# Two orders of small work in a mixture-of-experts stage, and the place of one constant's load

## The chip, the cores and the metric

The kernel runs on one core of a Trainium2 chip. The metric is device time in microseconds (us) of one execution. TensorE (PE) multiplies matrices, VectorE (DVE) and ScalarE (ACT) work element by element, GpSimd (POOL) does a few small steps, and SyncE (SP) issues nearly all DMA transfers; POOL issues some.

## The reference, cut to what matters

A decoder trunk of two layers on 256 tokens of width 1024, in float32. Each layer is a mixer (`w_in`, three head groups, `w_out`) and a feed-forward part: dense in layer 0, eight experts in layer 1, of which each token uses two.

```python
def _swiglu(t, w_g, w_u, w_d):
    return (jax.nn.silu(t @ w_g) * (t @ w_u)) @ w_d

def _moe(h, w_router, w_g, w_u, w_d):
    ...
    logits = (t @ w_router).astype(jnp.float32)
    top_v, top_i = lax.top_k(logits, TOP_K)
    top_w = jax.nn.softmax(top_v, axis=-1)
    gates = jnp.sum(jax.nn.one_hot(top_i, N_EXPERTS, dtype=jnp.float32) * top_w[..., None], axis=1)
    out = jnp.zeros(t.shape, jnp.float32)
    for e in range(N_EXPERTS):
        out = out + gates[:, e:e + 1] * _swiglu(t, w_g[e], w_u[e], w_d[e]).astype(jnp.float32)
    return out.astype(h.dtype).reshape(B, S, D)
```

Ahead of the router stands an RMS norm with weights of its own (1024 numbers), and a final norm follows the last layer.

## The kernel before

**Weights.** The experts' weights come as 264 chunks of 1 MB, 33 for each expert (11 of gate, 11 of up, 11 of down). Each chunk goes through four steps: a DMA from SP's queue into `w`, `wx` or a borrowed area (line 148), a rounded copy `wr` by ScalarE and the rest `wl = w - wr` by VectorE (`split`, lines 125 and 127), and matmuls with both halves. Float32 precision comes from three products for an even expert (lines 184 to 186, 12 matmuls a chunk) and from two for an odd one, whose tokens' two halves lie side by side (lines 887, 888, 956, 957; 8 matmuls a chunk). Every fourth chunk uses `wrx` and `wlx`, the others share a ring of three. So a chunk's split can start when TensorE is done with the chunk four before. A chunk's split is written in the program three chunks ahead of its matmuls (`AHEAD = 3`).

**Pairs.** The experts are ranked by their number of tokens and handled in pairs: expert 2p with 128 rows, 2p + 1 with 64 rows (`FEW`); what doesn't fit is left to a loop at the end (`rest`). The chunks of the odd expert run `LAG = 2` steps behind those of the even one, and the two are interleaved, gate, up and down, in the loop over `j`.

**Small tasks.** Between chunks run small tasks, the `jobs`:
- for pair 0 `count`, `order`, `assign` (which sets the ids from which SP addresses the later experts' weights), `where`, `shares` and `limits`, all short steps on VectorE;
- `marks`, one-hot matrices of a pair's tokens (VectorE, line 807, tile `xg`);
- `factors`, the tokens' shares (4 matmuls into `rgb`, line 841, then VectorE); `back`, transposed marks (TensorE into `ptb`, ScalarE out of it);
- `pick`, four a pair: gathers two of the eight slices of the tokens (8 matmuls into `gb`, line 821), and splits them into `xg`. For pairs 1 to 3 that is ScalarE, VectorE, ScalarE, VectorE; for pair 0 only the odd expert's columns are left to do, by one step on each;
- `scale` (two an expert), the expert's result times its shares into `yg`, and `finish` (four an expert), which scatters it (`cb`) and adds it to `h` (VectorE, line 977);
- `space` only takes memory.

`chunk()` appends a chunk to the list `prog` and then takes one job from the front of `jobs`. New jobs are put at the end when an expert's last down chunk is listed (`lower`), and when the memory of a pair is free (`collect`). Ahead of an even expert's first chunk all `pick` jobs still in the list, and what stands ahead of them, are listed at once. What is left at the end of the loop follows the last chunk. `in_order()` then fixes the order of the instructions of TensorE, VectorE and ScalarE as they were written. So the order of jobs is the order in which the engines meet them, and an engine that waits for one holds all behind it.

Before the change, the chunk numbers behind which the jobs stand are: pair 0, chunks 0 to 12; pair 1, chunks 30 to 39 (`space`, two `marks`, two `factors`, `back`, four `pick`); pair 2, 94 to 103; pair 3, 160 to 169; `scale` and `finish` of expert 6, 255 to 260. Expert 2's first chunk is 52, expert 4's 118, expert 6's 184, and the last chunk is 263.

**Constants.** `late_consts()` is called in layer 0's mixer; it starts the loads of `wa2` and `stg` from POOL's queue. `moe()` opens with the tile `gains`, the norm's weights repeated on all 128 partitions (512 KB), and its load from POOL's queue; POOL multiplies by it in front of the router.

Of the kernel before, what the change touches and what calls it, by code (L numbers as in the profile page):

```python
# [8 lines left out]
F32 = mybir.dt.float32  # L9
# [8 lines left out]
P = 128  # L18
T = 256
TT = 2  # L20
D = 1024
# [24 lines left out]
K_GAIN = K_TRI + 128  # L46
# [66 lines left out]
def trunk_kernel(ctx: ExitStack, tc: tile.TileContext, x, w_in, w_out, dense_w_gate, dense_w_up, dense_w_down,  # L113
                 moe_w_gate, moe_w_up, moe_w_down, final_norm_g, consts, decay_w, out):
    nc = tc.nc
# [4 lines left out]
    mix = early.enter_context(tc.tile_pool(name="mix", bufs=1))  # L120
# [72 lines left out]
    def tmp(shape, name, tag="tmp", bufs=5, dt=F32):  # L193
        pool = area["scratch"] if tag in ("tmp", "u", "cf_acc", "S", "r", "v", "gy", "qk", "sx", "kept", "fold", "rt_f") else sb
        return pool.tile(shape, dt, name=name, tag=tag, bufs=2 if tag == "tmp" and area["spare"] else bufs)

    def bank(shape, name):
        return ps.tile(shape, F32, name=name, tag="ps")
# [22 lines left out]
    mk = mix.tile([P, NL, P], U8, name="mk")  # L221
    mst = mix.tile([P, 9, P], F32R, name="mst")
    wa2 = mix.tile([17, 2, 256], F32, name="wa2")

    cr = cp.tile([P, 2, P], F32R, name="cr")
    oner, trir = cr[:, 0], cr[:, 1]
# [2 lines left out]
    def late_consts():  # L229
        nc.gpsimd.dma_start(wa2, decay_w)  # L230
        stg = tmp([P, 11 + NL, P], "stg", tag="E", bufs=1)
        nc.gpsimd.dma_start(stg, consts[:, K_M:K_GAIN].rearrange("p (l q) -> p l q", q=P))
        return stg

    def cast_consts(stg):
# [94 lines left out]
    def mixer(l, accs):  # L330
# [26 lines left out]
        if l == 0:  # L357
            stg = late_consts()
# [285 lines left out]
        return accs  # L644

    def moe(l, j, accs):
        gains = mix.tile([P, D], F32, name="gains")
        nc.gpsimd.dma_start(gains, bass.AP(tensor=consts.tensor, offset=consts.offset + K_GAIN, ap=[[0, P], [1, D]]))
        fh = tmp([P, 2, KT * T], "fh", tag="A", bufs=1)
        ft = fh[:, 0].rearrange("p (k t) -> p k t", k=KT)  # L650
        hg = fh[:, 1].rearrange("p (t d) -> p t d", t=TT)
# [80 lines left out]
        def places():  # L732
            cnt, rank, idf, few, room = (tmp([P, NE], n, tag="rt_" + n, bufs=1)
                                         for n in ("cnt", "rank", "idf", "few", "room"))
            w0 = cmp[:, 0, 0:NE]
            w1 = cmp[:, 1, 0:NE]
            to = cmp[:, 0, NE:2 * NE]
            V = nc.vector

            def count():  # L740
                nb = bank([P, NE], "nb")
                for tt in range(TT):
                    nc.tensor.matmul(nb, oner, msk[:, tt], start=(tt == 0), stop=(tt == 1))
                V.tensor_copy(cnt, nb)

            def order():
                lte = lt.rearrange("p (a b) -> p a b", b=NE)
                mine = cnt[:, :, None].broadcast_to([P, NE, NE])
                V.tensor_tensor(w0, cnt[:, None, :].broadcast_to([P, NE, NE]), mine, op=ALU.subtract)
                V.scalar_tensor_tensor(w1, w0, 0.0, lte, op0=ALU.is_equal, op1=ALU.mult)  # L750
                V.scalar_tensor_tensor(w0, w0, 0.0, w1, op0=ALU.is_lt, op1=ALU.add)
                V.tensor_reduce(rank, w0[:, :, 1:NE], axis=AX.X, op=ALU.add)
                V.memset(rank[:, 0:1], -1.0)

            def assign():
                V.tensor_tensor(to, target[:, :, None].broadcast_to([P, NE, NE]),
                                rank[:, None, :].broadcast_to([P, NE, NE]), op=ALU.is_equal)
                V.tensor_tensor(w0, to, iota[:, None, 0:NE].broadcast_to([P, NE, NE]), op=ALU.mult)
                V.tensor_reduce(idf, w0, axis=AX.X, op=ALU.add)
                V.tensor_scalar(ids, idf, -1.0, None, op0=ALU.add)  # L760

            def move(tt, src, dst):
                V.tensor_tensor(w0, to, src[:, None, :].broadcast_to([P, NE, NE]), op=ALU.mult)
                V.tensor_reduce(dst, w0, axis=AX.X, op=ALU.add)

            def where():
                for tt in range(TT):
                    move(tt, pos[:, tt], placed[:, tt])

            def shares():  # L770
                for tt in range(TT):
                    move(tt, gr[:, tt, :, 0], gp[:, tt, :, 0])
                V.tensor_copy(gp[:, :, :, 1], rs[:, :, None].broadcast_to([P, TT, NE]))
                V.tensor_tensor(folded, ident[:, 0:FEW], ident[:, FEW:P], op=ALU.add)

            def limits():
                V.tensor_scalar(few, rank, -0.5, None, op0=ALU.is_gt)
                V.scalar_tensor_tensor(few, rank, 3.5, few, op0=ALU.is_lt, op1=ALU.mult)
                V.tensor_scalar(room, few, float(FEW - P), float(P), op0=ALU.mult, op1=ALU.add)
                V.tensor_tensor(over, pos, room[:, None, :].broadcast_to([P, TT, NE]), op=ALU.subtract)  # L780
                V.tensor_tensor(few, cnt, room, op=ALU.subtract)
                V.tensor_scalar(few, few, 0.0, None, op0=ALU.max)
                V.tensor_reduce(nmax, few, axis=AX.X, op=ALU.max)

            return count, order, assign, where, shares, limits
# [73 lines left out]
        def width(c):  # L859
            return 512 if c < 5 else 256  # L860

        jobs = []

        def chunk(e, src, n, a, b, fn):
            prog.append(((e, src, n, a, b), fn))
            if jobs:
                step(*jobs.pop(0))

        def step(fn, *args):
            prog.append((None, partial(fn, *args)))  # L870

        def proj(which_src, e, c):
# [18 lines left out]
            for k0 in range(0, KT, kn):  # L891
                chunk(e, src, 2 * c + k0 // kn, kn, n, partial(run, k0))
# [89 lines left out]
        def item(kind, k):  # L982
            return items[kind][k] if 0 <= k < len(items[kind]) else None

        def lower(it):
            if it is None:
                return
            e, c = it
            for k2 in range(width(c) // 256):
                down(e, c, k2)  # L990
            if c == 5 and e < NE - 1:
                jobs.extend([(scale, e, (0,)), (scale, e, (1,))])
                jobs.extend((finish, e, (tt,), (nh,)) for nh in range(2) for tt in range(TT))
                if e % 2 == 1 and e < NE - 3:
                    collect(e // 2 + 2)

        def collect(p):
            jobs.extend([(space, p), (marks, p, 0), (marks, p, 1)])
            jobs.extend([(factors, p, 0), (factors, p, 1), (back, p)])
            jobs.extend((pick, p, 0, P + FEW, (k2,)) for k2 in range(KT // 2))  # L1000

        jobs.extend((fn,) for fn in places())
        jobs.extend([(marks, 0, 1), (factors, 0, 1), (back, 0)])
        jobs.extend((pick, 0, P, P + FEW, (k2,)) for k2 in range(KT // 2))
        n_pairs = len(items[0]) + LAG
        for j in range(n_pairs + 2):
            hv, hv1 = item(0, j), item(0, j - 1)
            lt_, lt1, lt2 = (item(1, j - LAG - d) for d in range(3))
            closing = j == n_pairs - 1
            if j == 4:  # L1010
                collect(1)
            if hv and hv[1] == 0 and j:
                while any(job[0] is pick for job in jobs):
                    step(*jobs.pop(0))
            if hv:
                drain = proj(0, *hv)
                if j == 0:
                    step(factors, 0, 0)
                step(drain)
            if lt1:  # L1020
                step(fold, *lt1)
            if j == 1:
                step(turn, *hv1)
            if not closing:
                lower(lt2)
            if lt1:
                step(unfold, *lt1)
            if hv:
                step(proj(1, *hv))
            if lt_:  # L1030
                step(proj(0, *lt_))
            lower(hv1)
            if hv and j:
                step(turn, *hv)
            if lt_:
                step(proj(1, *lt_))
            if closing:
                lower(lt2)
# [115 lines left out]
    accs = dense_ffn(0, 0, accs)  # L1154
    accs = mixer(1, accs)
    nmax, rest, close = moe(1, 0, accs)

    def final(close=None):
# [52 lines left out]
```

## Time and profile before

| | |
|---|---|
| time, median of 3 runs | 1185.08 us (1184.42 to 1187.38) |
| profiled execution | 1185.49 us, span of its trace 1183.5 us |
| mean granted TensorE clock | 0.985 |
| TensorE busy | 1138.0 us (96%) |
| VectorE, ScalarE busy | 990.5, 789.5 us |
| experts' first chunk starts | 450.26 us |
| first matmul of the last chunk | 1168.39 us |

The rows below are of the profiled execution. `start us` counts from the start of the span. A releaser in brackets is what ended the idle time in front of an instruction, and a clock of 1.00 is the full one. Neighbouring instructions of one kind are merged in a timeline's row (`x4`); then the time is that of all of them.

### The profile page before, as it was taken

The page shows a single profiled execution, that of the slowest core. Times are in us where ns is not written, and L with a number is a line of the kernel's source. Part 1 is how long each engine was busy: PE and PEld are TensorE (multiplying, and loading weights), DVE is VectorE, ACT ScalarE, POOL GpSimd, SP SyncE. Part 2 cuts the span into 40 slices and gives each one's busy share as a digit, 9 for nine tenths or more (in the row PEclk, how much of TensorE's full clock was granted, in tenths as well). Part 3 has the DMA queues.
Part 4 walks back from the last instruction along what each step waited for, and adds up shares of the span by engine and source line. Part 5 has one row for each costly group of instructions (what it writes and reads, how often), then busy time and mean ns, then how long its engine had stood idle before and what let it go on. Part 6 is the DMA issues. An engine that isn't in the chain of part 4 may idle for free.

```text
span 1183.5 us, 17163 instructions
## 1 busy us (share of the span) xinstructions
PE 1138.0 (96%) x6633; PEld 992.4 (84%) x6633; DVE 990.5 (84%) x1065; ACT 789.5 (67%) x801; POOL 28.0 (2%) x36
## 2 busy tenths in 40 slices
PE   6999999999899999899999999899999899999995
PEld 6998999999899978788888888788888788888883
DVE  4998655555679876799799999799999799999996
ACT  4754544334455466587688887688887788887874
POOL 2001000000000120000000000000000000000000
PEclk9999999999999998999999999999999999999999
DMA  9333555455433455898799999799999799999991
GB/s 374 128 138 146 191 189 191 179 183 180 155 129 140 179 218 210 321 373 314 265 416 423 408 424 385 284 400 424 402 424 382 293 411 423 401 424 401 425 403 38
DMA packets 48934, 348.97 MB, mean 295 GB/s; under 512 B 5447, under 2 KB 5447, under 8 KB 7120
## 3 DMA queue, kind: packets, MB, share of 16 engines
q1 hardware_dynamic: 48384, 345.50, 74.2%
q0 software_dynamic: 464, 2.33, 0.5%
q8 instruction: 54, 0.88, 0.3%
q14 instruction: 32, 0.26, 0.1%
HBM read 346.76 MB, written 1.05 MB: 294 GB/s over the span
## 4 chain that ended last, share of the span: by engine, by line
PE 80%; DVE 10%; issue 4%; ACT 4%; DMA 1%; POOL 0%; SPq 0%; POOLq 0%; DVEq 0%; ACTq 0%
PE gu L184 9%; PE gu L185 9%; PE gu L186 9%; PE acc_y L184 6%; PE acc_y L185 6%; PE acc_y L186 6%; DVE wl L127 5%; PE gu L888 5%; PE gu L887 5%; PE fb L929 3%; PE acc_y L956 3%; PE acc_y L957 2%; ACT wr L125 2%; DVE wlx L127 2%; PE sbk L443 1%
## 5 line engine op out<-in xcount | busy, mean ns | idle before, releaser
L127 DVE TENSOR_TENSOR wl<-w,wr 128x2048 fp32r<-128x2048 f32 (+2 forms) x267 | 464.1, 1759 | 76.9 <-ACT wr L125 76.5
L125 ACT ACTIVATE wr<-w 128x2048 fp32r<-128x2048 f32 (+2 forms) x267 | 391.9, 1491 | 187.5 <-issue 112.1
L127 DVE TENSOR_TENSOR wl<-wx,wr 128x2048 fp32r<-128x2048 f32 x54 | 122.9, 2284 | 13.4 <-ACT wr L125 13.3
L185 PE MATMUL gu<-wl,xg 128*128 128x512 f32 (+1 forms) x296 | 111.8, 378 | 2.1 <-DVE wl L127 2.1
L184 PE MATMUL gu<-wr,xg 128*128 128x512 f32 (+1 forms) x296 | 113.3, 383 | 0.4 <-ACT wr L125 0.4
L186 PE MATMUL gu<-wr,xg 128*128 128x512 f32 (+1 forms) x296 | 111.7, 377 | 0.0
L888 PE MATMUL gu<-wl,xg 128*128 128x512 f32 (+1 forms) x288 | 104.9, 372 | 3.3 <-DVE wl L127 3.3
L887 PE MATMUL gu<-wr,xg 128*128 128x512 f32 (+1 forms) x288 | 106.5, 377 | 1.1 <-ACT wr L125 1.1
L127 DVE TENSOR_TENSOR wlx<-w,wrx 128x2048 fp32r<-128x2048 f32 x45 | 102.7, 2283 | 4.3 <-ACT wrx L125 4.1
L125 ACT ACTIVATE wr<-wx 128x2048 fp32r<-128x2048 f32 x54 | 102.7, 1912 | 4.9 <-PE acc_y L186 2.2
L184 PE MATMUL gu<-f,wr 128*128 128x256 f32 x336 | 95.1, 283 | 0.0
L185 PE MATMUL gu<-f,wr 128*128 128x256 f32 x336 | 95.0, 283 | 0.0
L186 PE MATMUL gu<-f,wl 128*128 128x256 f32 x336 | 95.0, 283 | 0.0
L184 PE MATMUL acc_y<-wr,hr 128*128 128x512 f32 x228 | 90.7, 398 | 0.0
L186 PE MATMUL acc_y<-wr,hl 128*128 128x512 f32 x228 | 90.6, 397 | 0.0
L185 PE MATMUL acc_y<-wl,hr 128*128 128x512 f32 x228 | 90.5, 397 | 0.0
L125 ACT ACTIVATE wrx<-w 128x2048 fp32r<-128x2048 f32 x45 | 86.3, 1918 | 2.8 <-ACT wr L125 1.1
L185 PEld LDWEIGHTS gu<-wl,xg 128*128 128x128 f32 x296 | 57.1, 193 | 12.6 <-DVE wl L127 2.6
L184 PEld LDWEIGHTS gu<-wr,xg 128*128 128x128 f32 x296 | 57.1, 193 | 10.7 <-ACT wr L125 0.8
L186 PEld LDWEIGHTS gu<-wr,xg 128*128 128x128 f32 x296 | 56.9, 192 | 10.4
L888 PEld LDWEIGHTS gu<-wl,xg 128*128 128x128 f32 x288 | 54.3, 189 | 13.0 <-DVE wl L127 4.3
L185 PEld LDWEIGHTS gu<-f,wr 128*128 128x128 f32 x336 | 64.4, 192 | 0.4
(341 smaller groups left out, 2432.6 us busy)
## 6 DMA issues: line engine op xcount, KB each, us to landing
w<-in_moe_w_gate_dram SPq DMA_DIRECT2D x64, 1024.0 KB, 7.5
w<-in_moe_w_up_dram SPq DMA_DIRECT2D x60, 1024.0 KB, 7.7
w<-in_moe_w_down_dram SPq DMA_DIRECT2D x59, 1024.0 KB, 7.6
wx<-in_moe_w_down_dram SPq DMA_DIRECT2D x25, 1024.0 KB, 7.8
wx<-in_moe_w_gate_dram SPq DMA_DIRECT2D x24, 1024.0 KB, 7.5
wx<-in_moe_w_up_dram SPq DMA_DIRECT2D x23, 1024.0 KB, 7.2
w<-in_w_in_dram SPq DMA_DIRECT2D x20, 1024.0 KB, 4.7
w<-in_dense_w_gate_dram SPq DMA_DIRECT2D x11, 1024.0 KB, 4.8
```

The costliest lines, as they stand in the source:

```text
L125: i0 = nc.scalar.activation(r, src, AF.Copy, scale=scale)
L127: i1 = nc.vector.tensor_tensor(l, src, r.bitcast(F32), op=ALU.subtract)
L184: nc.tensor.matmul(o, sr, mr, start=start, stop=False)
L185: nc.tensor.matmul(o, sr, ml, start=False, stop=False)
L186: nc.tensor.matmul(o, sl, mr, start=False, stop=stop)
L443: nc.tensor.matmul(o, a0, a1, start=True, stop=True)
L887: nc.tensor.matmul(o, xg[:, 2, kt], wr[:, i], start=(kt == 0), stop=False)
L888: nc.tensor.matmul(o, xg[:, 2, kt], wl[:, i], start=False, stop=(kt == KT - 1))
L929: nc.tensor.matmul(b[:, n, i], kept[n][:, i * P:(i + 1) * P], X[e // 2][4], start=True, stop=True)
L956: nc.tensor.matmul(Y[e][nh], hb, wr[:, i, cs], start=first, stop=False)
L957: nc.tensor.matmul(Y[e][nh], hb, wl[:, i, cs], start=False, stop=fin)
```

## The change

1. The tile `gains` is made when the other tiles of that pool are, and its load is emitted in `late_consts()`, behind that of `stg`.
2. The jobs of pair 0 come in another order. The marks for the odd expert stand after `where`, then `shares` and the four picks; `factors`, `back` and `limits` follow.
3. A counter decides when `chunk()` takes a job: after each chunk as before, and from the loop's step `j == 3` (chunk 20) after every second.

By the new order the jobs stand behind these chunks: pair 0, 0 to 12 again; pair 1, 31 to 49 (every second one, `space` at 31, the picks at 43, 45, 47 and 49); pair 2, 101 to 117, picks at 113, 115 and 117, and the fourth directly behind the third, ahead of chunk 118; pair 3, 167 to 183 in the same way, and the fourth ahead of chunk 184; `scale` and `finish` of expert 6, 255, 257, 259, 261 and 263, with the last `finish` also behind chunk 263.

```diff
--- before.py
+++ after.py
@@ -221,6 +221,7 @@
     mk = mix.tile([P, NL, P], U8, name="mk")
     mst = mix.tile([P, 9, P], F32R, name="mst")
     wa2 = mix.tile([17, 2, 256], F32, name="wa2")
+    gains = mix.tile([P, D], F32, name="gains")
 
     cr = cp.tile([P, 2, P], F32R, name="cr")
     oner, trir = cr[:, 0], cr[:, 1]
@@ -230,6 +231,7 @@
         nc.gpsimd.dma_start(wa2, decay_w)
         stg = tmp([P, 11 + NL, P], "stg", tag="E", bufs=1)
         nc.gpsimd.dma_start(stg, consts[:, K_M:K_GAIN].rearrange("p (l q) -> p l q", q=P))
+        nc.gpsimd.dma_start(gains, bass.AP(tensor=consts.tensor, offset=consts.offset + K_GAIN, ap=[[0, P], [1, D]]))
         return stg
 
     def cast_consts(stg):
@@ -644,8 +646,6 @@
         return accs
 
     def moe(l, j, accs):
-        gains = mix.tile([P, D], F32, name="gains")
-        nc.gpsimd.dma_start(gains, bass.AP(tensor=consts.tensor, offset=consts.offset + K_GAIN, ap=[[0, P], [1, D]]))
         fh = tmp([P, 2, KT * T], "fh", tag="A", bufs=1)
         ft = fh[:, 0].rearrange("p (k t) -> p k t", k=KT)
         hg = fh[:, 1].rearrange("p (t d) -> p t d", t=TT)
@@ -859,11 +859,12 @@
         def width(c):
             return 512 if c < 5 else 256
 
-        jobs = []
+        jobs, beat = [], {"n": 0, "every": 1}
 
         def chunk(e, src, n, a, b, fn):
             prog.append(((e, src, n, a, b), fn))
-            if jobs:
+            beat["n"] += 1
+            if jobs and beat["n"] % beat["every"] == 0:
                 step(*jobs.pop(0))
 
         def step(fn, *args):
@@ -999,14 +1000,17 @@
             jobs.extend([(factors, p, 0), (factors, p, 1), (back, p)])
             jobs.extend((pick, p, 0, P + FEW, (k2,)) for k2 in range(KT // 2))
 
-        jobs.extend((fn,) for fn in places())
-        jobs.extend([(marks, 0, 1), (factors, 0, 1), (back, 0)])
+        count, order, assign, where, shares, limits = places()
+        jobs.extend([(count,), (order,), (assign,), (where,), (marks, 0, 1), (shares,)])
         jobs.extend((pick, 0, P, P + FEW, (k2,)) for k2 in range(KT // 2))
+        jobs.extend([(factors, 0, 1), (back, 0), (limits,)])
         n_pairs = len(items[0]) + LAG
         for j in range(n_pairs + 2):
             hv, hv1 = item(0, j), item(0, j - 1)
             lt_, lt1, lt2 = (item(1, j - LAG - d) for d in range(3))
             closing = j == n_pairs - 1
+            if j == 3:
+                beat["every"] = 2
             if j == 4:
                 collect(1)
             if hv and hv[1] == 0 and j:
```

## Rows read from the trace of the kernel before

**Rows 1.** The page, its first table: busy time by engine.
```profile
PE 1138.0 (96%) x6633; PEld 992.4 (84%) x6633; DVE 990.5 (84%) x1065; ACT 789.5 (67%) x801; POOL 28.0 (2%) x36
```

**Rows 2.** Stretches: length, then busy of PE, PEld, DVE, ACT, POOL; clock, DMA, GB/s.
```profile
475.90:500.00 24.10, 20.49 (x106) 17.36 (x106) 18.04 (x21) 11.74 (x11) 0.00 (x0) 0.93 0.87 324
...
560.00:600.00 40.00, 37.66 (x205) 32.35 (x204) 32.16 (x26) 29.50 (x30) 0.00 (x0) 0.96 0.79 298
600.00:700.00 100.00, 100.00 (x488) 83.62 (x487) 97.67 (x61) 82.98 (x64) 0.00 (x0) 1.00 1.01 419
...
736.00:765.00 29.00, 25.31 (x134) 21.05 (x132) 21.58 (x19) 18.76 (x20) 0.00 (x0) 0.94 0.76 284
...
916.00:945.00 29.00, 25.27 (x141) 20.98 (x140) 21.74 (x19) 19.28 (x22) 0.00 (x0) 1.00 0.76 291
```

**Rows 3.** TensorE waits, 450:500, 550:605, 695:765: us, times, longest.
```profile
PE rgb L841 <- DVE xg L807: 3.6, 1, 3.6
...
PE gu L185 <- DVE wl L127: 1.9, 1, 1.9
...
PE gu L888 <- DVE wlx L127: 1.8, 1, 1.8
```

**Rows 4.** TensorE timeline 470:503: start, us, line, tile, [idle before].
```profile
479.66 0.58 PE L841 MATMUL rgb<-gp,xg 128*128 128x2 f32 x4 [3.61 <-DVE xg L807]
...
482.18 0.63 PE L185 MATMUL acc_y<-wl,hr 128*128 128x512 f32 x1
...
499.08 0.98 PE L821 MATMUL gb<-xg,xt 128*128 128x64 f32 x8
499.89 0.47 PE L184 MATMUL gu<-wr,xg 128*128 128x512 f32 x1
```

**Rows 5.** VectorE timeline 468:500.
```profile
471.94 0.22 DVE L763 TENSOR_TENSOR cmp<-cmp,gr 128x64 f32<-128x64 f32 x1
...
475.26 0.17 DVE L777 TENSOR_SCALAR few<-rank 128x8 f32<-128x8 f32 x1
...
476.44 0.68 DVE L127 TENSOR_TENSOR hl<-tb,hr 128x512 fp32r<-128x512 f32 x1
...
479.23 0.48 DVE L807 TENSOR_SCALAR xg<-kc,placed 128x128 fp32r<-128x128 f32 x2
```

**Rows 6.** VectorE timeline 736:757.
```profile
742.76 0.42 DVE L127 TENSOR_TENSOR xg<-gb,xg 128x256 fp32r<-128x256 f32 x1
...
745.32 2.29 DVE L127 TENSOR_TENSOR wl<-wx,wr 128x2048 fp32r<-128x2048 f32 x1 [0.85 <-ACT wr L125]
...
750.27 2.29 DVE L127 TENSOR_TENSOR wl<-wx,wr 128x2048 fp32r<-128x2048 f32 x1 [1.69 <-ACT wr L125]
```

**Rows 7.** ScalarE timeline 736:757.
```profile
743.21 0.28 ACT L125 ACTIVATE xg<-gb 128x128 fp32r<-128x128 f32 x1 [2.42 <-DVE xg L127]
```

**Rows 8.** TensorE timeline: first matmuls of chunks 74 and 86.
```profile
664.24 0.39 PE L184 MATMUL gu<-wr,xg 128*128 128x512 f32 x1
...
693.12 0.39 PE L184 MATMUL gu<-wr,xg 128*128 128x512 f32 x1
```

**Rows 9.** TensorE timeline 1160:1183.5.
```profile
1168.39 0.50 PE L956 MATMUL acc_y<-wrx,hb 128*128 128x512 f32 x1 [2.37 <-DVE hb L127]
```

**Rows 10.** VectorE timeline 1160:1183.5.
```profile
1166.80 0.68 DVE L977 TENSOR_TENSOR h<-h,cb 128x512 f32<-128x512 f32 x1
...
1168.05 0.29 DVE L127 TENSOR_TENSOR hb<-s,hb 128x128 fp32r<-128x128 f32 x1 [0.38 <-ACT hb L125]
1170.35 0.75 DVE L129 SCALAR_TENSOR_TENSOR yg<-acc_y,rg,yg 128x512 fp32r<-128x512 f32 x1 [2.01 <-ACT yg L125]
```

**Rows 11.** Timeline of all engines 0:14.
```profile
2.01 0.57 POOL L648 DMA_DIRECT2D gains<-in_consts_dram  x1
...
11.40 2.00 ACT L125 ACTIVATE wr<-w 128x1024 fp32r<-128x1024 f32 x2 [4.08 <-DMA w<-in_w_in_dram]
...
13.01 0.59 POOL L232 DMA_DIRECT2D stg<-in_consts_dram  x1 [3.48 <-ACT wr L125]
```

## What I expect of the change

> **What bounds the kernel now.** I read the busy times first: TensorE works 96% of the span, VectorE 84% [rows 1]. So only three things can give time back: a stretch in which TensorE idles, one in which its clock is low, and the two ends of the program. The table by stretch places them [rows 2]. From 600 to 700 us nothing can be won: TensorE is busy for the whole 100 us at clock 1.00, with the DMA engines full and VectorE at 97.67. Four stretches of the expert stage are different, and each holds small tasks:
>
> - A, 475.9 to 500 (first pair of experts): idle 24.10 − 20.49 = 3.6 us; clock 0.93, which costs 0.07 × 24.1 = 1.7. Together 5.3.
> - B, 560 to 600 (gathers for pair 1): idle 2.3, clock 0.96, or 1.6. Together 3.9.
> - C, 736 to 765 (pair 2): idle 3.7, clock 0.94, or 1.7. Together 5.4.
> - D, 916 to 945 (pair 3): idle 3.7, clock 1.00. Together 3.7.
>
> In all 18.3 us, which is the most that a better order of the small tasks could win. The waits say what ends the idle time [rows 3]: in A one wait of 3.6 us, for the one-hot marks (`xg`, line 807); in B, C and later the wait for a weight chunk's low half (`wl`, line 127). TensorE's timeline shows that the 3.6 us are one piece, with low-clock matmuls 2.5 us behind it [rows 4]: a 128x512 matmul takes 0.63 us there and 0.39 at full clock [rows 8], so this is the lower of the levels 1.2 and 2.4 GHz.
>
> **A: the new order for pair 0.** Before, VectorE does the shares (four steps from 471.94 and two small ones), one `wl` of 2.2 us, seven small steps of `limits` from 475.26, `hl` at 476.44, another `wl`, and only at 479.23 the marks [rows 5]; `factors` on TensorE stands behind them and holds chunk 8. With the change the marks take the shares' place, 471.94, and the shares go where `limits` was. Two picks fill TensorE between chunks 6 and 8 (0.81 us each, from 499.08 to the next instruction at 499.89; the row merges the pick's eight matmuls into one of 0.98) [rows 4], and `factors` follows chunk 10. Chunk 8 then waits for `hl`. That is still behind the shares, four steps at 0.25 and two small ones, 1.2 us in place of the 1.2 of `limits`, and one 0.28 copy of the pick: I put it between 475.7 and 476.7, when TensorE, whose chunk 7 ends at 476.05 (479.66 − 3.61), still has the picks to do until 477.6. The 3.6 us go, and with them the low-clock spell: −5.3, less 0.1 for a few tenths at `back`, whose transposes now follow `factors` by one chunk: −5.2. Bounds: −5.3, and −1.7 if a new wait of the same 3.6 stood at `back` and only the spell went. I take the near end: VectorE, on which `back` would wait, is busy for 18.04 of the 24.10 us of A [rows 2], and it runs ahead of TensorE there.
>
> **B, C and D: one task per two chunks.** In C the copies are the bound [rows 6, 7]: `wl` starts at 745.32 and the next at 750.27, 4.95 us a chunk. ScalarE's second pick copy waits 2.42 us for VectorE's first, which stands behind the `wl` before it, and the next `wr` stands behind that copy. So a pick chains `wr`, `wl`, the 0.42 and the 0.28 in a row, on two engines that otherwise overlap. TensorE's need is smaller: in a stretch without tasks, chunk 74 starts at 664.24 and chunk 86 at 693.12 [rows 8], 28.88/12 = 2.41 a chunk, and a pick of 192 columns adds about 0.9 (an estimate from the 0.81 for 64). So each pick puts the copies 4.95 − 3.3 = 1.6 us further behind, 6.6 for four. Idle 3.7 came of it, so the lead that the copies had, and could spend, was 2.9.
>
> With one task per two chunks, two chunks and a pick take 4.95 + 2.2 = 7.15 on the copies (2.2 is a `wl` that waits for nothing, the row's 2.29 less its overlap with what follows) and 2 × 2.41 + 0.9 = 5.7 on TensorE: behind by 1.4 a pick. In B that is 4 × 1.4 − 2.9 = 2.8 of idle, in small pieces, and half of the old low-clock spell (0.8): 3.6 against 3.9, −0.3 (bounds −3.9, nothing lost, and +2, a spell more). In C and D there is less room. Expert 4's first chunk is 118, and pair 2's task list only begins with `space` after chunk 101 (after 94 before): one job is still unserved at chunk 118, and the loop that serves all picks ahead of an expert's first chunk flushes it, so picks three and four run with no chunk between them. The fourth costs a chain of 2.7 against 0.9, 1.8. That makes 3 × 1.4 + 1.8 − 2.9 = 3.2 us of idle each, and in one piece, at chunk 119 (185 for pair 3), whose input is the last group. Before, C and D idled 7.4 together, with one spell of 1.7: 9.1. After: 6.4, and again one spell of the two possible, since C and D were alike in idle and only one fell: 8.1. So −1.0 (bounds −2.7 with no spell, +0.7 with two).
>
> Scales and finishes are spread out too. They cost nothing where TensorE now runs at 100 of 100 us, as from 600 to 700 [rows 2], where finishes run; the cover is the copies' lead of 2.9 us, and a chain of one 0.68 add per two chunks is half of what VectorE carries now.
>
> **Tail.** The finishes of expert 6 move back: two (0.68 on VectorE each, as at 1166.80) fall behind the last chunk. Of the four adds ahead of `hb` two go, so `hb` (1168.05, for which TensorE idles 2.37 until 1168.39 [rows 9]) comes up to 1.2 us sooner; then the two adds and their matmuls stand before the last `yg` (1170.35, which today waits for ScalarE alone) [rows 10]: 0.5 for the first matmuls, 1.3 for the adds: +1.75. Net +0.5 (0 to +1.4).
>
> **Late issue of `gains`.** Today it is issued at 2.01 us, though the program emits it only in `moe`, long after `stg`, which is issued at 13.01; the first chunk's `wr` at 11.40 waits 4.08 for its DMA [rows 11]. So the order of lines on GpSimd's queue is not what sets this: an issue that waits for nothing goes out early. The diff adds no wait, so I expect it still near 2 us, at no price and no gain. If it does go out behind `stg`, 0.5 MB less stand ahead of the first weights: at 419 GB/s [rows 2] that is 1.25 us at most, covered or not. I take 0, range −1.25 to 0. Its reader is layer 1's routing, behind the dense layer and a whole mixer, which cover the landing either way. The tile's place in memory moves too, and with it which weight load waits for its last reader; none of the waits of TensorE in the expert stage [rows 3] names a transfer, so that is 0 as well. The Trainium skill, DMA: Bandwidth & Descriptors, section "Issuing engines are not separate DMA queues", says that transfers started from different engines share the 16 DMA engines and interleave; by that rule a really late issue would give −1.25 rather than 0. The 4.08 us wait fits it, but no run here shows the other case.
>
> **Sum.** −5.2 − 0.3 − 1.0 + 0.5 + 0 = −6.0, against this execution's 1185.49 (span 1183.5): 1179.5; the execution lies 0.4 above the median 1185.08, so 1179.1.
>
> **Rivals.**
> R1, the spells multiply. The stalls at 119 and 185 come in one piece, of 3.2 us, near the 3.6 of A that was followed by the low clock. If both trigger it, and B keeps its old price, A's gain is partly lost: −5.2 + 0 + 0.7 + 0.5 = −4.0, or −2.0 with B at its upper bound: 1181 to 1183 by the median, and 1185 if A's new order leaves another 2 us of wait, as one `wl` ahead of `back` would. For it: a single piece in A had a spell. Against: D lost 3.7 without one. The Trainium skill, TensorE: Matmul & The Clock Gate, section "HAM oscillation — how this bites in real kernels", says that idle waits let the array's clock fall to half, so that they cost twice; D's rows do not agree for pieces below 2 us, A's do for one of 3.6.
> R2, the gathers become free. If ScalarE can slip its second `wr` ahead of the pick's second copy, nothing chains: two chunks and a pick take 2 × 2.29 + 0.7 = 5.3 on VectorE, under TensorE's 5.7. Then C and D give their 9.1, and B its 3.9 at most: −5.2 − 9.1 − (0 to 3.9) + 0.5 = −13.8 to −17.7, or 1167.4 to 1171.3; half of it leads to 1175.5. For it: ScalarE gets a chunk without a pick between two picks. Against: the engines' order is written by hand, and a chunk's split always follows.
> R3, slower: the flushed pick holds expert 4 and 6's first chunk itself. Place: chunk 118 and 184, TensorE waiting for `xg`. At 8 us and a spell of 1.7 each that is 19.4 against C and D's present 9.1, +10.3; with −5.0 from the rest +5.3: 1190.4. It decides (slower by 3.6) from 7.2 us of idle at each, over twice what I worked out. Against: the fourth pick's chain is 2.7, and chunk 118 needs only the groups before it.
> That the change does not do what it says holds for `gains` alone, and is in the forecast.
>
> **Chances and range.** Forecast (1175.5 to 1181.5) 0.52; R1 0.24; R2 0.15; R3 0.09. No change is what lies within 0.3%, 3.6 us, which a measurement here can hardly tell: 1181.5 to 1188.6. R1 falls there nearly whole: faster 0.67, same 0.25, slower 0.08. The range leaves out R3 and most of R2: 1173.5 to 1186.0.
>
> **What would show it.** A: no wait on line 807, clock 1.00 from 475.9 to 500, chunk 14 about 5 us earlier. C and D: one piece of idle near 3 us just ahead of chunk 119 and 185, with or without a spell; R2 shows TensorE at 100% there, R3 a wait for `xg` of 8 us. The tail: two `cb` groups behind the last chunk. Start: `gains` still near 2.0 us. I am wrong if new idle shows at `back`, or the picks' wait of 2.42 on ScalarE is gone.

## The result, and the profile after

The changed kernel takes 1178.26 us (median of 5 runs, 1177.67 to 1178.87), the kernel before 1185.08 beside it: a ratio of 0.9936, with a 95% interval of 0.9922 to 0.9950. That is 6.8 us, or 0.6%, faster; 1179.1 was predicted. The profiled execution takes 1178.44 us, with a span of 1176.6.

TensorE's share of the span, 96% before [rows 1], is 97%:

```profile
PE 1135.7 (97%) x6633; PEld 989.5 (84%) x6633; DVE 991.0 (84%) x1065; ACT 788.6 (67%) x801; POOL 28.1 (2%) x36
```

The stretches that answer to [rows 2] (length, then busy PE, PEld, DVE, ACT, POOL; clock, DMA share, GB/s; a chunk stands 1.4 to 17 us earlier than before, so the limits differ):

```profile
470.00:495.00 25.00, 25.00 (x133) 21.33 (x132) 21.85 (x24) 16.38 (x15) 0.00 (x0) 1.00 0.98 391
...
550.00:612.00 62.00, 58.00 (x306) 48.35 (x305) 52.15 (x41) 44.66 (x42) 0.00 (x0) 0.97 0.89 354
...
736.00:765.00 29.00, 29.00 (x171) 25.43 (x170) 28.16 (x25) 21.44 (x19) 0.00 (x0) 1.00 1.01 418
765.00:790.00 25.00, 22.96 (x114) 18.97 (x113) 18.61 (x17) 18.86 (x21) 0.00 (x0) 0.93 0.78 300
...
930.00:970.00 40.00, 37.96 (x198) 31.90 (x197) 33.23 (x29) 29.24 (x30) 0.00 (x0) 0.96 0.89 344
```

A (470 to 495) has no idle time and full clock, as forecast. The old stall in C (736 to 765) is gone too, but one stands behind it, at 765 to 790: 25.00 − 22.96 = 2.0 us idle and clock 0.93. D has the same at 930 to 970: 40.00 − 37.96 = 2.0 us idle, and 0.96 over 40 us is as much clock lost (1.6 us) as 0.93 over 25 (1.7). In B (550 to 612) 62.00 − 58.00 = 4.0 us are idle, where 2.3 were. TensorE's waits from 450 to 1100 us (total, times, longest) say the same; the 3.6 us for the marks [rows 3] are not among them:

```profile
PE gu L186 <- DVE xg L127: 4.1, 2, 2.0
PE gu L185 <- DVE wl L127: 1.8, 1, 1.8
PE gu L889 <- DVE wlx L127: 1.5, 1, 1.5
PE acc_y L185 <- DVE wl L127: 0.6, 1, 0.6
PE tb L918 <- DVE s L909: 0.5, 1, 0.5
```

The first line is the stall of C and D, once each; the lines with `wl` and `wlx` are B. TensorE's timeline of C shows it, in the middle of chunk 119, the chunk named in the prediction:

```profile
779.23 0.50 PE L186 MATMUL gu<-wrx,xg 128*128 128x512 f32 x1 [2.04 <-DVE xg L127]
...
780.63 0.63 PE L184 MATMUL gu<-wrx,xg 128*128 128x512 f32 x1
```

The wait is for the low half of a slice gathered by a pick, and the second row is a matmul at the low clock (0.63 us against 0.39 at the full one [rows 8]).

To find where the rest came from I timed the stretches between the first matmuls of fixed chunks, at which no small task is pending. This table is worked out from the traces (us; the experiments' names are explained below):

| kernel | experts start | A: chunks 0–14 | B: 30–60 | C: 88–126 | D: 154–192 | 255 to the end |
|---|---|---|---|---|---|---|
| before | 450.26 | 52.48 | 84.11 | 106.18 | 105.01 | 39.26 |
| changed | 447.73 | 47.33 | 86.15 | 103.97 | 104.11 | 41.09 |
| changed − before | −2.5 | −5.1 | +2.0 | −2.2 | −0.9 | +1.8 |
| changed, second trace | 450.55 | 47.12 | 86.16 | 103.96 | 104.11 | 40.98 |
| `gains_alone` | 449.03 | 52.44 | 84.12 | 106.14 | 105.01 | 39.49 |
| `order_alone` | 446.89 | 47.45 | 84.05 | 107.26 | 105.94 | 39.43 |
| `beat_alone` | 449.19 | 52.47 | 86.18 | 104.17 | 104.28 | 41.19 |
| `order_and_beat` | 450.21 | 47.06 | 86.15 | 103.97 | 104.11 | 41.28 |
| `gains_late` | 445.58 | 47.36 | 86.12 | 103.99 | 104.12 | 41.25 |
| `beat_not_tail` | 450.27 | 47.10 | 86.13 | 103.98 | 104.09 | 39.93 |
| `before_copies_first` | 446.85 | 54.01 | 79.32 | 100.18 | 100.18 | 40.52 |
| `copies_first` | 450.56 | 47.14 | 79.22 | 99.96 | 100.07 | 39.92 |
| `copies_first_each` | 448.93 | 47.04 | 79.40 | 100.15 | 100.14 | 40.89 |
| `best` | 447.04 | 47.02 | 79.40 | 100.14 | 100.15 | 39.36 |
| `best_spaced` | 445.90 | 47.08 | 79.22 | 99.96 | 100.07 | 41.24 |

The rest of the experts (14–30, 60–88, 126–154, 192–255) is equal within 0.1 us in all of them. Rows of one stretch in which the programs are alike repeat to 0.4 us or better, or differ by 0.9 to 1.6. Windows of 1 us show why: in such a pair one has a spell more of low clock (half of the full one), mostly 3.4 us long, that falls whole or in part into the stretch.

### The profile page after: what moved, and what is told of

The parts are those of the page before. It is cut to its first block, busy times and chain, and to the rows that moved or that the text cites. A ratio compares the mean times of both kernels' runs of the same rounds, so it can differ in the third digit from the quotient of the medians.

```text
span 1176.6 us, 17161 instructions
## 1 busy us (share of the span) xinstructions
PE 1135.7 (97%) x6633; PEld 989.5 (84%) x6633; DVE 991.0 (84%) x1065; ACT 788.6 (67%) x801; POOL 28.1 (2%) x36
## 4 chain that ended last, share of the span: by engine, by line
PE 88%; DVE 5%; ACT 3%; issue 2%; DMA 1%; POOL 0%; SPq 0%; POOLq 0%; ACTq 0%; DVEq 0%
PE gu L186 10%; PE gu L184 10%; PE gu L185 10%; PE acc_y L184 6%; PE acc_y L186 6%; PE acc_y L185 6%; PE gu L888 6%; PE gu L889 6%; DVE wl L127 3%; PE acc_y L957 3%; PE fb L930 3%; PE acc_y L958 3%; PE sbk L445 1%; ACT wr L125 1%; PE a_ps L191 1%
## 5 line engine op out<-in xcount | busy, mean ns | idle before, releaser
L185 PEld LDWEIGHTS gu<-wl,xg 128*128 128x128 f32 x296 | 57.1, 193 | 12.8 <-DVE wl L127 2.7
L185 PEld LDWEIGHTS gu<-f,wr 128*128 128x128 f32 x336 | 64.4, 192 | 0.4
L184 PEld LDWEIGHTS gu<-f,wr 128*128 128x128 f32 x336 | 64.4, 192 | 0.4
```

The source lines that it names most:

```text
L184: nc.tensor.matmul(o, sr, mr, start=start, stop=False)
L185: nc.tensor.matmul(o, sr, ml, start=False, stop=False)
```

## The experiments

Each was run 4 to 11 times, beside runs of the kernel before on the same chip. A ratio is to that kernel, with its 95% interval in brackets; a range behind a time is that of the runs.

**`gains_alone`**, **`order_alone`** and **`beat_alone`** put one part each of the change into the kernel before; the diffs are the three parts of the change.

> The kernel before with the load of the norm's weights moved, and nothing else. Theory 1 (the load does not matter: it is issued near 2.0 us in both traces): 1185 us, within 1 us of the kernel before, and the trace may or may not have the low-clock spell at 320 to 328 us, since that is chance. Rival (the 2.5 us by which the experts start earlier in the changed kernel come from the load): 1182.6 us, experts' first matmul at 447.7, spell at 320 us gone.

Measured: 1185.61 us against 1185.00, ratio 1.0005 (0.9996 to 1.0015). No effect beyond −0.5 to +1.8 us, so the load doesn't give the 2.5 us. It went out at 2.01 us, as it did in the changed kernel, whose rows these are:

```profile
2.01 0.57 POOL L234 DMA_DIRECT2D gains<-in_consts_dram  x1
...
11.85 2.00 ACT L125 ACTIVATE wr<-w 128x1024 fp32r<-128x1024 f32 x2 [4.67 <-DMA w<-in_w_in_dram]
...
13.52 0.59 POOL L233 DMA_DIRECT2D stg<-in_consts_dram  x1 [4.11 <-PE tp L274]
```

> The kernel before with the new order of pair 0's tasks alone. Theory 1 (the gain is this order's, worth the 5.4 us seen between chunks 4 and 14): 1179.7 us; no wait for the marks in A, low clock in A gone; B, C, D and the tail as in the kernel before. Rival (the gain is lost again to later waits, and the spacing of the tasks is what saves it): above 1182.

Measured: 1181.37 us, 0.9976 (0.9967 to 0.9985), 3.6 us faster, between the two theories. A gives 5.0 us in the table. In C and D one more spell each falls on the same idle pieces, and they are 1.1 and 0.9 us longer. TensorE's waits there are those of before (0.8, 1.0 and 1.8 us in C, 0.7, 1.1 and 1.8 in D):

```profile
PE gu L888 <- DVE wl L127: 3.3, 3, 1.8
PE gu L185 <- DVE wl L127: 1.9, 1, 1.9
PE gu L888 <- DVE wlx L127: 1.8, 1, 1.8
PE gu L887 <- ACT wr L125: 1.1, 1, 1.1
PE gu L887 <- ACT wrx L125: 1.0, 1, 1.0
```

With the early start that is −3.4 − 5.0 + 1.1 + 0.9 = −6.4, about what the profiled execution (1179.19 us, the fastest of the eleven) is below that of before, 6.3. The run at the median has a mean clock of 0.982 against the 0.986 of the profiled one, so it lost more to the low clock; where, no trace shows.

> The kernel before with one task per two chunks from j = 3, and nothing else. Theory 1 (the changed trace's own account: B +2.1, C -2.2, D -0.9, tail +1.8): 1185.9 us, within 1.5 of the kernel before. Rival (spacing gives a gain by itself): 1180 or less.

Measured: 1185.33 us, 1.0003 (0.9994 to 1.0012). Spacing alone is worth nothing that can be told from noise: its four terms in the table are +2.1, −2.0, −0.7 and +1.9, together +1.3, beside a start that is 1.1 earlier in this trace.

**`order_and_beat`** is the change without its first part, **`after_again`** the changed kernel once more ("second trace" in the table).

> The changed kernel without the move of the load of the norm's weights. In the first four traces the stages of the experts add up exactly (order of pair 0: -5.1 us; spacing: +2.1, -2.1, -0.8 and in the tail +1.8), but the time at which the experts start differs from 446.9 to 450.6 us by low-clock spells near 16 and 323 us. Theory 1 (that start is chance): 1179 to 1182 us, the middle of the runs over 1 us apart, stages of the experts as in the changed kernel within 0.2 us. Rival (the moved load, only together with the other parts, gives the 2.5 us): experts start at 450, 1181 us or more with little scatter.

> The changed kernel once more, to see how much of its 6.8 us is the time at which its experts start. Theory 1 (447.7 us was chance; without it the parts give 4.0 to 5.0): experts start between 445 and 451 us, the runs spread over more than the 1.2 us of the first five, median 1178 to 1181. Rival (it is a property of this kernel): start at 447.7 again, median 1178.3, spread as small.

Measured: 1179.73 us (1177.69 to 1180.75), 0.9940 (0.9927 to 0.9954); and 1179.47 us (1177.04 to 1180.88), 0.9943 (0.9930 to 0.9957). The experts of the same program started at 447.73 us in one trace and at 450.55 in the other. The windows of 310 to 335 us, at the beginning of layer 1, show what differs: first the trace of the prediction's result, then the second one, with the clock behind the column of POOL:

```profile
310.00:335.00 25.00, 21.81 (x149) 19.58 (x148) 14.74 (x23) 11.50 (x23) 2.81 (x5) 1.00 0.37 129
```

```profile
310.00:335.00 25.00, 21.81 (x128) 19.80 (x127) 13.95 (x22) 10.89 (x22) 2.82 (x5) 0.86 0.37 126
```

1.00 against 0.86, in the same program: (1 − 0.86) × 25 = 3.5 us of clock, or two spells. `order_alone` and `before_copies_first`, which change nothing ahead of the experts, started them at 446.89 and 446.85. So of the 6.9 us between the two first traces 2.5 are not shown to be the change's, and the first theory held.

**`copies_first`** changes one thing in the changed kernel, how a pick writes its slices:

```diff
-                if c0 == 0:
-                    split(b[:, :, 0:P], xg[:, 0, ks], xg[:, 1, ks])
-                if c1 > P:
-                    split(b[:, :, P:P + FEW], xg[:, 2, ks, 0:FEW], xg[:, 2, ks, FEW:P])
+                cuts = []
...
+                for src, hi, lo in cuts:
+                    nc.scalar.activation(hi, src, AF.Copy, scale=1.0)
+                for src, hi, lo in cuts:
+                    nc.vector.tensor_tensor(lo, src, hi.bitcast(F32), op=ALU.subtract)
```

> The changed kernel, but a pick of pairs 1 to 3 writes both ScalarE copies first and then both VectorE ones. Theory 1 (the stalls in B, C and D come from ScalarE's second copy waiting 2.4 to 2.8 us for VectorE's first, with the next weight copy behind it): that wait is gone, the 4.0, 2.0 and 2.0 us of idle and their three spells of 1.7 go, 13 us less: 1165 us. Rival (VectorE or the loads are the bound, whatever the order of a pick's copies): 1176 to 1178.5, the stalls remain.

Measured: 1162.99 us (1161.10 to 1164.88), 0.9810 (0.9796 to 0.9823): 22 us faster than the kernel before. In the changed kernel ScalarE's second copy of a pick waits for VectorE's first, which stands behind `wl`. ScalarE in B, changed kernel:

```profile
592.16 1.90 ACT L125 ACTIVATE wr<-w 128x2048 fp32r<-128x2048 f32 x1
593.96 0.38 ACT L125 ACTIVATE xg<-gb 128x256 fp32r<-128x256 f32 x1
597.16 0.28 ACT L125 ACTIVATE xg<-gb 128x128 fp32r<-128x128 f32 x1 [2.83 <-DVE xg L127]
```

and VectorE there:

```profile
594.50 2.28 DVE L127 TENSOR_TENSOR wl<-w,wr 128x2048 fp32r<-128x2048 f32 x1
596.71 0.42 DVE L127 TENSOR_TENSOR xg<-gb,xg 128x256 fp32r<-128x256 f32 x1
```

The copy at 597.16 is held for 2.83 us, and the next `wr` with it. Both steps read the tile `gb`, though they write different slices of `xg`; whether that is why the one must wait for the other, no run here shows. With the copies in the other order the two ScalarE copies (here merged, x2) run at once and `wr` follows them. ScalarE and VectorE of `copies_first`:

```profile
581.59 0.55 ACT L832 ACTIVATE xg<-gb 128x256 fp32r<-128x256 f32 x2 [1.15 <-PE gb L821]
582.02 3.73 ACT L125 ACTIVATE wr<-wx 128x2048 fp32r<-128x2048 f32 x2
```

```profile
580.91 2.29 DVE L127 TENSOR_TENSOR wl<-w,wr 128x2048 fp32r<-128x2048 f32 x1
583.11 0.62 DVE L834 TENSOR_TENSOR xg<-gb,xg 128x256 fp32r<-128x256 f32 x2
```

Its stretches B, C and D are full, at clock 1.00, and from 450 to 1125 us TensorE waits once, for 0.4 us:

```profile
560.00:612.00 52.00, 52.00 (x291) 44.98 (x290) 48.46 (x38) 41.93 (x40) 0.00 (x0) 1.00 0.99 391
735.00:790.00 55.00, 55.00 (x306) 47.54 (x305) 51.54 (x42) 44.59 (x42) 0.00 (x0) 1.00 0.99 393
890.00:960.00 70.00, 70.00 (x373) 59.84 (x373) 66.47 (x54) 56.98 (x50) 0.00 (x0) 1.00 0.99 390
```

```profile
PE tb L923 <- DVE s L914: 0.4, 1, 0.4
```

**`before_copies_first`** makes the same edit in the kernel before, and nothing else.

> The kernel before, with nothing changed but the order of a pick's copies (both of ScalarE, then both of VectorE). Theory 1 (that order alone caused the idle time in B, C and D, and A's 3.6 us are another matter): idle 2.3, 3.7 and 3.7 us there go with the spells of 1.7 that follow them (two in the kernel before, three or four in other traces), 9.7 + 3.4 to 6.8: 1169 to 1172 us; A keeps its 3.6 us wait. Rival (one pick per chunk still keeps VectorE behind): 1176 or more.

Measured: 1170.19 us (1168.97 to 1170.47), 0.9872 (0.9857 to 0.9887). Waits from 440 to 1100 us:

```profile
PE rgb L846 <- DVE xg L807: 3.6, 1, 3.6
PE gb L821 <- DVE xg L805: 0.6, 1, 0.6
PE tb L922 <- DVE s L913: 0.5, 1, 0.5
```

B, C and D are free with one task per chunk as well, so the pick's inner order was their cause; A's 3.6 us stand, now with two spells where there was one (A 54.01 in the table, not 52.48).

**`copies_first_each`** is `copies_first` with `beat["every"]` left at 1.

> The kernel with both ScalarE copies of a pick first, but one task per chunk as before, everything else as changed. Theory 1 (once ScalarE no longer waits for VectorE inside a pick, the spacing is worth nothing in B, C and D and its cost in the tail goes): 1161.2 us, 1.8 below the spaced version's 1163.0, no wait of TensorE in B, C, D. Rival (the spacing is what keeps VectorE's pick work off the path): waits for `wl` return in B, C and D, 1166 us or more.

Measured: 1163.78 us (1162.95 to 1166.17), 0.9812 (0.9798 to 0.9825): the same as the spaced one, and no waits in B, C, D. The 1.8 us in the tail that I expected did not come.

**`beat_not_tail`** sets `beat["every"] = 1` when expert 6's scale is listed.

> The changed kernel, but from expert 6's scale and finish on one task per chunk again. Theory 1 (spacing costs 1.8 us in the tail, since two finishes fall behind the last chunk): 1176.5 us, and the stretch from chunk 255 to the end 39.3 us as in the kernel before, not 41.1. Rival (the tail's length is set by the low clock, wherever the finishes stand): 1178.3, stretch 41.

Measured: 1179.09 us, 0.9932 (0.9919 to 0.9946), no difference from the changed kernel. The last stretch is 39.93 us, 1.2 shorter and between the two theories, but this execution's experts started at 450.27. In total time it is inconclusive.

**`gains_late`** makes the load really late, and **`best`** and **`best_spaced`** join it to the new copies, one task per chunk and one per two (but one per chunk in the tail).

```diff
-        nc.gpsimd.dma_start(stg, consts[:, K_M:K_GAIN].rearrange("p (l q) -> p l q", q=P))
-        nc.gpsimd.dma_start(gains, bass.AP(tensor=consts.tensor, offset=consts.offset + K_GAIN, ap=[[0, P], [1, D]]))
+        first = nc.gpsimd.dma_start(stg, consts[:, K_M:K_GAIN].rearrange("p (l q) -> p l q", q=P))
+        with behind((first,)):
+            nc.gpsimd.dma_start(gains, bass.AP(tensor=consts.tensor, offset=consts.offset + K_GAIN, ap=[[0, P], [1, D]]))
```

> The changed kernel with the load of the norm's weights held behind that of `stg` on GpSimd's queue, so that it really goes out late. Theory 1 (0.5 MB less ahead of the first weights is 1.25 us at most): the first weight copy starts 0.5 to 1.2 us earlier than at 11.85, and the time falls by that, 1177 to 1178. Rival (another load, kc or h, holds the first copy): no change, 1178.3.

Measured: 1176.85 us (1175.32 to 1178.42), 0.9922 (0.9909 to 0.9936). Its start:

```profile
9.62 2.00 ACT L125 ACTIVATE wr<-w 128x1024 fp32r<-128x1024 f32 x2 [2.51 <-DMA w<-in_w_in_dram]
...
12.55 0.60 POOL L233 DMA_DIRECT2D stg<-in_consts_dram  x1 [3.22 <-ACT a L278]
...
13.15 0.54 POOL L235 DMA_DIRECT2D gains<-in_consts_dram  x1
```

The first weight copy begins at 9.62 us (9.29 and 9.38 in the two versions below); in the traces with the load at 2.0 us it begins between 10.85 and 11.85. So the first weights land at least 1.2 us sooner, and 2.2 against the changed kernel; in the total the intervals still overlap that of the changed kernel.

> Copies of a pick in the new order, pair 0's tasks in the changed order, one task per chunk, and the load of the norm's weights held behind that of `stg`. Theory 1 (the parts add): 1163.8 - 1.4 = 1162.4 us; first weight copy near 9.6 us. Rival (the start's gain is lost in the mixer, which is bound elsewhere): 1163.8.

> As the one before, but one task per two chunks from j = 3 to expert 6's scale, and one per chunk behind it. Theory 1 (with the copies in the new order the spacing is worth nothing either way): within 0.7 us of it. Rival (spacing still pays by smoothing the copies): 1 us or more faster.

Measured: 1161.24 us (1158.62 to 1162.83), 0.9794 (0.9780 to 0.9807), and 1162.68 us (1160.80 to 1162.81), 0.9804 (0.9791 to 0.9817). `best` has the lowest median, 2.1% below the kernel before; the two are not told apart.

## Why the prediction was right, point by point

The total was right by its largest term, A, and otherwise by luck: B came out 2.3 us worse than forecast and C with D 2.1 better, and the tail's 1.3 too much was covered by the earlier start, which was not forecast. Term by term, against the profiled executions:

- **A, −5.2.** Measured −5.1. The marks' wait and the spell behind it went, and `back` brought no new wait. This is the step that the forecast rested on, and `order_alone` shows it by itself.
- **B, −0.3 (bounds −3.9 to +2).** Measured +2.0, at the bound. The kind of stall was right, its size not: 4.0 us idle and a whole spell, where 2.8 and half a spell were expected. The step that failed is TensorE's need of 5.7 us for two chunks and a pick. It came from a mean over both kinds of chunks; of chunks 43 to 46 three are the odd expert's short ones, and these four with two picks take 10.3 us (570.30 to 580.62), 5.2 for two chunks and a pick. The copies took 7.3 (the low halves of chunks 47, 49, 51 and 53 start at 577.52, 584.83, 592.29 and 599.54), close to the 7.15 of the forecast.
- **C and D, −1.0 (bounds −2.7 to +0.7).** Measured −3.1, outside the bounds. The place was right (chunk 119, and 185), and each had one spell, which was R1's way; but the stall is 2.0, not 3.2. The lead is the mis-sized term: `wl` of chunk 116, written just ahead of the first pick's copies, ended at 764.12, 4.0 us before that chunk's first matmul, and 3 × 1.4 + 1.8 − 4.0 = 2.0. VectorE and TensorE of the changed kernel:

```profile
761.84 2.28 DVE L127 TENSOR_TENSOR wl<-w,wr 128x2048 fp32r<-128x2048 f32 x1
```

```profile
768.15 0.48 PE L888 MATMUL gu<-wr,xg 128*128 128x512 f32 x1
```

  The 2.9 had been worked out from the same mean need of TensorE. In the kernel before the lead could be read, and was 4.6 us at C's first pick (chunk 103, 738.06 to 742.62):

```profile
735.78 2.28 DVE L127 TENSOR_TENSOR wlx<-w,wrx 128x2048 fp32r<-128x2048 f32 x1
```

```profile
742.62 0.42 PE L887 MATMUL gu<-wrx,xg 128*128 128x512 f32 x1
```

- **Tail, +0.5 (0 to +1.4).** Measured +1.8, outside the bounds. `hb` comes only 0.6 sooner (1.78 us of idle ahead of the last chunk against 2.37 [rows 9]), and the low clock falls on what follows:

```profile
1158.01 0.50 PE L957 MATMUL acc_y<-wrx,hb 128*128 128x512 f32 x1 [1.78 <-DVE hb L127]
...
1161.04 1.58 PE L976 MATMUL cb<-yg,xg 128*128 128x512 f32 x4
1163.46 2.47 PE L976 MATMUL cb<-yg,xg 128*128 128x512 f32 x8 [0.84 <-ACT yg L125]
```

  The last chunk takes 1161.04 − 1158.01 = 3.0 us, 2.0 before; the four `cb` matmuls 1.58, against 1.09 in `copies_first`. That is 1.5 of the 1.8. Whether the spell falls there goes with the execution: the last stretch of `copies_first`, spaced as well, is 39.92 us. So in this trace 0.3 is left for the finishes themselves.
- **`gains`, 0.** Right: issued at 2.01 us before and after. The bound for a really late issue, 1.25 us, was a little low for the first copy (1.2 to 2.2, by the trace that it is compared with). The trace agrees with the rule of the Trainium skill that the prediction weighed (DMA: Bandwidth & Descriptors, "Issuing engines are not separate DMA queues"), by which transfers started from different engines share the same DMA engines: holding back GpSimd's load sped up SyncE's (first copy at 9.62 us).

The terms measured give −5.1 + 2.0 − 2.2 − 0.9 + 1.8 = −4.4, and the earlier start −2.5: −6.9. The second trace, with the late start, took 1180.88 us, 4.6 below the profiled execution of before. But the two sets of five runs of the changed kernel have medians 1178.26 and 1179.47, 6.8 and 6.1 us below those of the kernel before beside them (1185.08 and 1185.59). `order_alone` suggests why: with an early start (446.89) C and D, unchanged, had 2.0 us more of spells. So the kernel before may gain less from an early start than the changed one. How often each starts early stays open, since only one run of each set has a trace. The mean clocks hint that the first five were lucky: 0.985 in the trace with the early start and 0.984 in the other four, but 0.982 in the trace with the late start and 0.982 to 0.987 in the four beside it.

R2 did not happen, and the reason given against it was right. Its condition, that nothing chains inside a pick, is what `copies_first` made true: R2 expected 2 × 2.29 + 0.7 = 5.3 us of VectorE for two chunks and a pick to be enough, and the stalls vanished. The 18.3 us that the prediction called the most that an order could win were too few: in `copies_first` A, B, C and D are 5.3, 4.9, 6.2 and 4.9 us shorter than before, 21.4 together. In B, C and D that is 0.8 to 1.2 us more than the idle time and the clock of the windows account for, and no run shows what the rest is.

## What to carry to other kernels

Ask why two engines that share a queue of small steps wait for each other before spreading the steps out: the order of four copies in a task was worth 15 us by itself (`before_copies_first`), their spacing nothing. Compare stretches between fixed points of the work, not total times, where the clock shifts a run by 2 to 3 us. And read from the trace when an instruction is issued: a load moved in the program, without a new wait, went out at the same 2.01 us.

## What was not expected of the hardware

Between the experts' start and their last chunk the low clock came in spells of 3.4 us, or of twice that, in all these traces (windows of 1 us show them; the one of 13.7 us that begins ahead of the experts is left out), and the same idle pieces were followed by one spell, by more, or by none: D of the kernel before had 3.7 us of idle in pieces of up to 1.8 and clock 1.00 [rows 2]; `order_alone`, with the same waits, had a spell there. After a single piece of 2.0 us, C and D had one in all six traces with that stall. The start of layer 1 had two, one or none in executions with the same work, and two cost 2.8 us there (447.73 against 450.55).
